# Another order of the steps of a two-branch scan on one core

## Chip, cores and metric

One core of a Trainium2 chip runs the whole kernel as one launch. The metric is the device time of one execution in microseconds, as the median of several runs.

## What is computed

One layer of a diffusion backbone on 1152 tokens (128 context, 1024 latent) of width 1024. The reference, cut to the order of its stages:

```python
h = rmsnorm(x, n1) * (1.0 + sc1) + sh1
proj = jnp.einsum('bld,de->ble', h, w_in_l).astype(jnp.float32)
# group A, 4 heads: gated linear recurrence, both directions
hg_out = head_rmsnorm(merge_heads(hg_outs[0] + hg_outs[1]), HG_HEADS, hg_norm_w_l) * jax.nn.silu(hg_g)
# group B, 4 heads: mLSTM on depthwise-convolved q/k, both directions
ml_out = head_rmsnorm(merge_heads(ml_outs[0] + ml_outs[1]), ML_HEADS, ml_norm_w_l) * jax.nn.sigmoid(ml_o)
mix = jnp.concatenate([hg_out, ml_out], axis=-1).astype(h.dtype)
x = x + g1 * jnp.einsum('ble,ed->bld', mix, w_out_l)
h = rmsnorm(x, n2) * (1.0 + sc2) + sh2
x = x + g2 * ((jax.nn.silu(h @ w_gate_l) * (h @ w_up_l)) @ w_down_l)
```

The modulation vectors sh, sc and g come from one more matrix product with the conditioning.

## The kernel before

Tokens lie in three ranges r of 384. Weights and activations are split into a high and a low part, and a product is three matmuls (`three`, line 135). The first part normalises the tokens, computes the first modulation and multiplies the first weight unit. The scan part does the eight heads and the rest of the modulation, then comes the output projection, and a long feed-forward part in two passes ends the kernel.

The first and the scan part are cut into some 130 and 450 steps, written out by hand in two lists, `ORDER0` and `ORDER` (lines 48 to 87). A loop runs each list: a step's name picks a function, which issues that step's instructions on all engines and queues. The lists set the order in which work is handed over; where a step needs a tile whose pool has no free buffer, or data that are not there, its instructions stand behind that on their engine, and the program's builder may place later steps' instructions ahead of them. Each engine then runs its own instructions in a fixed order, and so does each queue (SP for nearly all loads, POOL for the stores of head outputs).

The steps of an HGRN head (`g.h.`): zq, zf, zb, zg project one range each (24 matmuls, line 135, into tiles of that name; line 333 for the first unit); L builds decays and the scores within chunks (many small operations on DVE, tiles lv and of); KV updates the states (tile tk); O multiplies scores and states with the values (tile o) and calls `head_norm`; F calls `head_out`.

The steps of an mLSTM head (`m.h.`): zm projects q or k; cv is the convolution on DVE (tile qk); zo projects the output gate (tile og); KV updates the states (tiles mtk, C); E loads two 384 KB tiles, eb and qt, from the rows of the gates in DRAM, broadcast over the partitions (line 861, SP's queue); O1 multiplies q and k (tile ps) and turns eb into weights; O2 multiplies with values and states (tile mo, lines 891 and 893) and calls `head_norm`; F calls `head_out`. The normed tile `on` lies between the two:

```python
def head_norm(idx, r, src):
    on = s15("on" + nm, "on", 2).rearrange("p (c t) -> p c t", c=3)
    ...
def head_out(idx, r, nw, gate):
    E.transpose(pt[:, c, :], on[:, c, :], ident)
    ...
    G.dma_start(mix_d[idx, :, r * TR:(r + 1) * TR], mx)
```

`head_norm` squares on ACT, takes the root on POOL and scales on ACT (line 397). `head_out` transposes on PE (tile pt, line 405), applies weight and gate in place on DVE and stores from POOL's queue. The pool holds two `on` tiles, four Q tiles (eb and qt of the E steps) and three gate tiles, shared by zg and zo.

Other steps: vload loads and splits a weight unit for the values and vproj multiplies it (tile pv); late.k multiplies part k of the second modulation (four loads of 256 KB through two tiles wm, line 196 on PE) and lateb.k hands it on; gates is the row work for the mLSTM gates (Exp and Ln on ACT, in between Sigmoid of the heads); wo.k loads and splits row block k of the output weights, out.i.q loads head outputs and om.i.n.q multiplies them (line 984). Every first projection of a unit (zq.0, zb.0, zm.0.0, zo.0 of heads 0 and 2) and every vload issues four loads of 256 KB on SP's queue and their splits on ACT and DVE.

Of the kernel before, what the change touches and what calls it, by code (L numbers as in the profile page):

```python
# [45 lines left out]


ORDER0 = """
x.0 x.1 x.2 norm.0 norm.1 norm.2 x.3 norm.3 x.4 x.5 x.6 norm.4 raw.0 norm.5 split.0 mod.0 raw.1 mod.1 x.7
mrow.0 mod.2 h.0.0 mrow.1 h.0.1 mm.0.0.0 x.8 mm.0.0.1 mod.3 mm.0.1.1 norm.6 h.1.0 norm.7 h.1.1 split.1  # L50
mm.0.1.0 norm.8 mm.1.1.0 mrow.2 h.2.0 mod.4 raw.2 h.0.2 mm.1.0.1 mrow.3 mod.5 h.1.2 mm.0.0.2 h.2.1 h.3.2 h.3.1
mm.2.0.1 h.2.2 mm.1.1.1 mod.6 mrow.4 h.4.2 mm.2.1.1 mm.0.1.2 mm.1.1.2 h.4.0 mod.7 mrow.5 raw.3 h.4.1 h.3.0
h.5.1 mm.1.0.2 split.2 mm.2.1.2 mm.3.1.1 mm.3.0.1 mm.1.0.0 mm.2.1.0 mm.2.0.2 h.5.2 h.5.0 mrow.6 mm.2.0.0
mm.3.0.2 mm.4.0.2 h.6.1 mm.4.0.1 mm.3.1.2 split.3 mm.3.0.0 mm.3.1.0 mm.5.0.2 mrow.7 mm.4.1.0 h.6.2 h.7.2 h.6.0
mm.5.1.0 mm.4.1.2 mm.4.0.0 mm.5.0.0 mm.4.1.1 mm.5.1.1 h.7.0 mm.6.1.1 mm.5.0.1 mm.6.0.2 mm.5.1.2 mm.7.0.2
mm.6.1.2 mm.6.1.0 h.7.1 mm.6.0.1 mm.6.0.0 mm.7.0.1 mm.7.0.0 mm.7.1.2 mm.7.1.1 mm.7.1.0
"""
# [1545 lines left out]
```

## Time and profile before

| | us |
|---|---|
| median of 3 runs (1671.05 to 1676.36) | 1672.95 |
| the profiled execution | 1671.47 |
| its span, first to last instruction | 1669.7 |
| PE busy in the span | 1595.8 |
| DVE busy | 1195.0 |
| ACT busy | 694.8 |

PE is the engine of the matmuls, DVE of the elementwise work on vectors, ACT of the activations, POOL a second small vector engine, SP the queue of loads. Times in the profile count from the first instruction. A wait is named as the engine, tile and line that waited, an arrow, and what ended the wait; a line such as L135 is that of a helper, so the tile's name says which step it is.

### The profile page before, as it was taken

What the parts mean: (1) busy time and instruction counts of PE and PEld (TensorE: products, weight loads), DVE (VectorE), ACT (ScalarE), POOL (GpSimd) and SP (SyncE); (2) the same over time, 40 slices, a digit from 0 to 9 for tenths busy, and PEclk for the clock granted to TensorE, in tenths of its full rate; (3) what the DMA queues carried; (4) which work ended last, traced back from release to release, by engine and by line L of the source; (5) the groups of instructions that cost most, each with busy time, mean ns of one, the idle gap of its engine ahead of it and who ended that gap; (6) DMA issues with size and microseconds to landing.
All of it is one profiled execution on the core that took longest, in us unless ns stands there. A gap on an engine that the chain in (4) does not pass through costs nothing.

```text
span 1669.7 us, 31305 instructions
## 1 busy us (share of the span) xinstructions
PE 1595.8 (96%) x11993; PEld 1437.8 (86%) x11993; DVE 1195.0 (72%) x2620; ACT 694.8 (42%) x1656; POOL 155.5 (9%) x264
## 2 busy tenths in 40 slices
...
GB/s 316 121 24 70 83 57 88 42 72 56 77 169 50 104 90 76 96 167 191 143 184 240 214 197 200 182 191 196 183 202 233 199 232 244 256 232 239 241 207 102
DMA packets 123467, 261.53 MB, mean 157 GB/s; under 512 B 12444, under 2 KB 39476, under 8 KB 122292
## 3 DMA queue, kind: packets, MB, share of 16 engines
...
## 4 chain that ended last, share of the span: by engine, by line
PE 77%; issue 7%; DMA 6%; DVE 6%; ACT 2%; POOL 1%; SPq 0%; another core or an unknown queue 0%; DVEq 0%; POOLq 0%; ACTq 0%
PE gu L1285 27%; PE dn L135 15%; PE po L984 5%; PE zm L135 4%; PE pv L135 4%; PE zg L135 3%; PE zb L135 3%; PE zf L135 2%; DMA wm<-in_dram 2%; PE z L333 2%; PE lm L196 1%; PE zo L135 1%; DMA qt<-rows_d 1%; PE zq L135 1%; PE lv L510 1%
## 5 line engine op out<-in xcount | busy, mean ns | idle before, releaser
L135 PE MATMUL dn<-hid 128*128 128x512 f32 x1188 | 307.2, 395 | 6.6 <-ACT hid L1292 5.2
L135 PEld LDWEIGHTS dn<-hid 128*128 128x128 f32 x1188 | 214.3, 189 | 43.9 <-ACT hid L1292 6.2
L1285 PE MATMUL gu<-s,Tb 128*128 128x320 f32 (+1 forms) x1584 | 235.3, 297 | 0.6 <-ACT Tb L1096 0.4
L1285 PEld LDWEIGHTS gu<-s,Tb 128*128 128x128 f32 x1584 | 222.7, 191 | 6.3 <-ACT Tb L1096 0.7
L125 DVE TENSOR_TENSOR tmp<-gu,tmp 128x320 f32<-128x320 f32 (+1 forms) x308 | 136.0, 453 | 72.9 <-PE gu L1285 70.7
L1096 ACT CAST Tb<-r 128x512 fp32r<-128x512 f32 x176 | 106.7, 619 | 143.3 <-PE gu L1285 79.3
L1285 PE MATMUL gu<-a,Tb 128*128 128x320 f32 (+1 forms) x1056 | 156.1, 296 | 0.0
L1285 PEld LDWEIGHTS gu<-a,Tb 128*128 128x128 f32 x1056 | 148.4, 190 | 3.7
L125 DVE TENSOR_TENSOR acc<-acc,dn 128x512 f32<-128x512 f32 x172 | 117.6, 684 | 22.5 <-PE dn L135 22.5
L119 DVE TENSOR_TENSOR Tb<-r,Tb 128x512 fp32r<-128x512 f32 x176 | 119.5, 687 | 17.1 <-ACT Tb L1096 14.1
L984 PE MATMUL po<-wo_A,mix 128*128 128x512 f32 x288 | 94.2, 402 | 0.5 <-ACT mix L213 0.5
L1255 ACT CAST hid<-raw_dn 128x512 fp32r<-128x512 f32 x88 | 52.6, 617 | 74.2 <-PE dn L135 62.9
L135 PE MATMUL pv<-wh_v,h_hi 128*128 128x256 f32 (+1 forms) x288 | 82.4, 286 | 0.0
L135 PE MATMUL pv<-wh_v,h_lo 128*128 128x256 f32 (+1 forms) x288 | 81.9, 284 | 0.0
L135 PE MATMUL pv<-wl_v,h_hi 128*128 128x256 f32 (+1 forms) x288 | 81.8, 284 | 0.0
L1285 PEld LDWEIGHTS gu<-s,Tt 128*128 128x128 f32 x528 | 74.7, 189 | 4.4 <-DVE Tb L119 1.1
L1285 PE MATMUL gu<-s,Tt 128*128 128x320 f32 (+1 forms) x528 | 77.4, 296 | 0.9 <-DMA Tt<-t_d 0.9
L1285 PEld LDWEIGHTS gu<-a,Tt 128*128 128x128 f32 x528 | 74.8, 189 | 3.6 <-ACT Tb L1096 0.3
L128 DVE SCALAR_TENSOR_TENSOR qk<-pad,sm,qk 128x384 f32<-128x384 f32 (+1 forms) x144 | 77.5, 567 | 0.3
L1285 PE MATMUL gu<-a,Tt 128*128 128x320 f32 (+1 forms) x528 | 77.4, 296 | 0.1
L168 POOL TENSOR_TENSOR rs_f<-ms_f,half 128x3 f32<-128x3 f32 x24 | 25.8, 1074 | 498.2 <-DVE ms_f L166 498.2
L119 DVE TENSOR_TENSOR hid<-raw_dn,hid 128x512 fp32r<-128x512 f32 x88 | 60.2, 686 | 13.3 <-ACT hid L1255 13.3
...
## 6 DMA issues: line engine op xcount, KB each, us to landing
r<-in_dram SPq DMA_DIRECT2D x154, 256.0 KB, 3.2
...
raw_dn<-in_dram SPq DMA_DIRECT2D x88, 256.0 KB, 3.2
...
wm<-in_dram SPq DMA_DIRECT2D x64, 256.0 KB, 3.7
...
```

What stands on the lines that cost most here:

```text
L119: V.tensor_tensor(out=out, in0=a, in1=b, op=ALU.subtract)
L125: V.tensor_tensor(out=out, in0=a, in1=b, op=ALU.add)
L128: V.scalar_tensor_tensor(out=out, in0=a, scalar=s, in1=b, op0=op0, op1=op1)
L135: E.matmul(ps, a, b, start=(i == 0), stop=(i == n - 1))
L168: G.tensor_tensor(out=rs, in0=ms, in1=half[:, 0:n], op=ALU.pow)
L196: E.matmul(ps[32 * j:32 * j + 32, :], cT[:, 4 * g + j, :], rhs, start=(g == 0), stop=(g == 1), tile_position=(0, 32 * j))
L333: E.matmul(first[b][r], x, y, start=(k == 0 and n == 0), stop=(k == KD - 1 and n == 2))
L510: E.matmul(lv[32 * j:32 * j + 32, c, lev, :], kc[:, b:b + 32], diag(Q, b, m, 32 // (2 * m)), tile_position=(0, 32 * j))
L984: E.matmul(ps[n], mt[:, a, k, :], b[:, k, nn], start=(k == 0 and m == 0), stop=(k == KD - 1 and m == 2))
L1096: S.copy(hi, src)
L1255: S.copy(hi, draw[u, n])
L1285: E.matmul(ps, rt[:, x, k, :], lt[:, y, k, :], start=(n == 0), stop=(n == 11))
```

## The change

Both lists are permuted; no step is added, left out or altered. In `ORDER`, in five of sixteen places the O or O2 of a range stands ahead of the F of the range before, where that was so nowhere. The gate projections m.0.zo.2 and m.2.zo.2 stand behind F.1 of their heads, m.2.zo.1 behind the KV steps. All E steps but m.0.E.2 and m.3.E.2 stand apart from their O1. late.13 and late.14 stand together, late.15 after m.3.F.1. L and vproj of the first heads, and the early loads and products in `ORDER0`, are permuted too.

```diff
-x.0 x.1 x.2 norm.0 norm.1 norm.2 x.3 norm.3 x.4 x.5 x.6 norm.4 raw.0 norm.5 split.0 mod.0 raw.1 mod.1 x.7
...
+h.0.0 x.7 mod.2 mrow.1 h.0.1 x.8 h.1.0 mm.0.1.0 mm.0.0.0 mm.0.0.1 mm.0.1.1 norm.6 norm.7 h.1.1 mm.1.0.1 mod.3
...
 ORDER = """
...
-g.1.zb.1 g.0.O.1 pads g.1.zq.2 g.1.zb.2 g.1.zg.0 g.0.F.1 lateb.1 g.1.zg.1 late.2.B g.1.L.0 g.0.O.2 lateb.2
-g.0.F.2 g.1.zg.2 g.1.L.1 g.1.KV.0 g.2.zq.0 g.1.L.2 g.2.zf.0 late.3.B g.2.zq.1 g.1.KV.1 g.1.KV.2 g.2.zf.1
...
-vproj.1.5 m.0.cv.1.0 m.0.cv.0.2 g.2.L.1 vproj.1.2 m.0.zm.1.2 vproj.1.8 m.0.cv.1.1 g.2.KV.0 gates g.2.L.2
-g.2.KV.1 g.3.zq.0 g.3.zq.1 g.3.zq.2 m.1.zm.0.0 g.3.zf.0 late.6.B g.2.KV.2 g.3.zf.1 g.3.zf.2 m.1.zm.0.1 g.2.O.0
-g.3.zb.0 lateb.6 g.3.L.0 g.3.states g.2.F.0 g.2.O.1 late.7.B lateb.7 g.2.F.1 m.0.cv.1.2 late.8.B g.3.zb.1
...
-vproj.2.3 g.3.O.1 m.0.zo.0 g.3.F.1 g.3.O.2 m.1.cv.1.0 m.0.reload vproj.2.0 m.0.zo.1 vproj.2.1 m.0.states
-vproj.2.4 vproj.2.2 g.3.F.2 m.0.zo.2 vproj.2.6 vproj.2.5 m.0.KV.0 lateb.10 late.11.B m.1.cv.0.1 m.1.cv.0.2
-vproj.2.7 m.0.KV.1 lateb.11 vproj.2.8 m.0.KV.2 m.0.E.0 m.0.O1.0 m.0.E.1 m.0.O1.1 m.0.O2.0 m.0.F.0 m.0.O2.1
-m.0.F.1 m.1.states m.1.cv.1.1 m.0.E.2 m.0.O1.2 m.0.O2.2 m.1.zo.0 m.0.F.2 m.1.KV.0 m.1.E.0 m.1.O1.0 m.1.cv.1.2
-m.1.KV.1 m.1.zo.1 m.1.KV.2 m.2.zm.0.0 m.2.zm.0.1 m.1.O2.0 m.1.zo.2 m.2.cv.0.0 m.2.zm.0.2 vload.3 m.2.zm.1.0
-m.1.E.1 m.1.O1.1 m.2.zm.1.1 m.2.zm.1.2 m.1.F.0 m.2.cv.0.1 vproj.3.6 m.1.E.2 m.1.O1.2 m.1.O2.1 m.2.cv.1.0
-vproj.3.3 vproj.3.0 vproj.3.1 m.2.cv.1.1 m.2.zo.0 vproj.3.7 m.1.F.1 m.1.O2.2 vproj.3.8 m.2.cv.0.2 vproj.3.4
-m.1.F.2 vproj.3.5 m.2.states m.2.zo.1 m.2.cv.1.2 m.2.zo.2 vproj.3.2 m.2.KV.0 m.2.E.0 m.2.O1.0 m.3.zm.0.0
-m.2.KV.1 m.2.KV.2 m.2.O2.0 m.2.F.0 m.3.zm.0.1 m.2.E.1 m.2.O1.1 m.3.zm.0.2 m.2.O2.1 m.3.zm.1.0 m.2.E.2 m.2.O1.2
-m.3.states late.12.A m.3.cv.0.0 m.3.zm.1.1 m.2.F.1 m.3.cv.0.1 m.2.O2.2 m.3.cv.1.0 m.3.zo.0 m.3.zm.1.2 m.3.KV.0
-m.3.zo.1 m.2.F.2 m.3.zo.2 m.3.cv.0.2 lateb.12 wo.0 m.3.cv.1.1 late.13.A m.3.KV.1 m.3.E.0 m.3.O1.0 m.3.cv.1.2
-m.3.KV.2 lateb.13 late.14.A m.3.O2.0 m.3.E.1 m.3.O1.1 m.3.F.0 lateb.14 nout m.3.E.2 m.3.O1.2 late.15.A lateb.15
-wo.1 wo.2 out.0.0 wo.3 m.3.O2.1 wo.4 out.1.0 om.0.0.0 out.2.0 om.0.1.0 m.3.F.1 m.3.O2.2 om.2.1.0 out.0.1 out.2.1
-wo.5 wo.6 wo.7 om.0.0.1 om.1.1.0 m.3.F.2 om.2.1.1 out.1.1 om.1.0.0 om.0.1.1 om.1.1.1 om.2.0.0 om.2.0.1 om.1.0.1
...
+g.0.KV.1 g.1.zf.0 vproj.0.8 g.0.KV.2 lateb.0 g.1.zf.1 g.1.zb.0 g.0.O.0 late.1.B g.1.zb.1 g.1.zq.2 g.0.O.1
+g.1.zf.2 g.0.F.0 g.1.zg.0 g.1.states g.0.F.1 g.1.L.0 lateb.1 late.2.B g.0.O.2 g.2.zq.0 g.1.KV.0 g.0.F.2 g.1.L.1
...
+g.2.zq.2 g.1.O.0 g.2.zb.1 g.2.states g.1.F.0 g.2.zf.2 lateb.3 late.4.B g.2.L.0 g.1.O.1 lateb.4 g.1.O.2 late.5.B
...
+m.0.cv.0.2 m.0.cv.1.0 vproj.1.0 g.2.L.1 vproj.1.2 m.0.cv.1.1 vproj.1.8 g.2.KV.0 g.3.zq.0 gates g.3.zq.1 g.2.L.2
+g.3.zf.0 m.1.zm.0.0 g.2.KV.1 g.3.zq.2 late.6.B g.2.KV.2 g.2.O.0 g.3.zf.1 g.3.zf.2 m.1.zm.0.1 lateb.6 g.3.zb.0
+g.2.F.0 g.3.L.0 late.7.B g.2.O.1 lateb.7 m.0.cv.1.2 g.2.O.2 late.8.B g.3.zb.1 g.3.zb.2 g.2.F.1 g.3.L.1 g.2.F.2
...
+g.3.O.1 g.3.zg.2 lateb.9 m.1.zm.1.1 vload.2 m.1.zm.1.2 late.10.B vproj.2.3 g.3.F.0 m.0.zo.0 m.1.cv.0.0 g.3.F.1
+g.3.O.2 m.0.reload vproj.2.5 m.0.states m.1.cv.0.1 m.0.zo.1 g.3.F.2 vproj.2.0 vproj.2.2 vproj.2.1 vproj.2.6
+lateb.10 late.11.B m.1.cv.1.0 m.0.KV.0 m.0.E.0 vproj.2.4 m.0.E.1 m.1.cv.1.1 m.0.O1.0 m.0.O1.1 vproj.2.8
+vproj.2.7 m.0.KV.1 m.0.KV.2 m.0.O2.0 lateb.11 m.0.O2.1 m.1.states m.1.KV.0 m.1.cv.0.2 m.0.F.0 m.1.cv.1.2 m.1.E.0
+m.1.KV.1 m.0.E.2 m.0.O1.2 m.0.F.1 m.1.zo.0 m.1.zo.1 m.1.O1.0 m.0.O2.2 m.0.zo.2 m.2.zm.0.0 m.0.F.2 m.1.zo.2
+vload.3 m.1.KV.2 m.2.zm.0.1 m.2.zm.0.2 m.1.E.1 vproj.3.7 m.2.zm.1.0 m.1.O2.0 m.2.cv.0.0 m.1.O1.1 m.2.zm.1.1
+m.2.cv.1.0 m.2.zm.1.2 m.1.F.0 m.2.cv.0.1 vproj.3.6 m.1.O2.1 vproj.3.1 m.2.cv.1.1 m.1.E.2 m.2.zo.0 m.2.E.0
+vproj.3.4 m.1.F.1 vproj.3.0 m.1.O1.2 m.2.cv.0.2 vproj.3.3 m.1.O2.2 vproj.3.5 vproj.3.8 m.1.F.2 m.2.cv.1.2
+vproj.3.2 m.2.states m.2.KV.0 m.2.KV.1 m.2.KV.2 m.2.O1.0 m.2.zo.1 m.2.O2.0 m.2.E.1 m.3.zm.0.0 m.3.zm.0.1 m.2.F.0
+m.3.zm.1.0 m.2.E.2 m.2.O1.1 m.3.zm.0.2 m.2.O2.1 m.3.zo.0 m.3.states m.2.O1.2 m.3.cv.0.0 m.3.cv.0.1 m.3.E.0
+m.3.zm.1.1 m.2.F.1 m.2.zo.2 m.2.O2.2 late.12.A m.3.zm.1.2 m.3.cv.1.0 m.3.KV.0 m.2.F.2 m.3.cv.0.2 m.3.zo.1
+m.3.cv.1.1 m.3.zo.2 m.3.E.1 m.3.KV.1 lateb.12 late.13.A lateb.13 late.14.A m.3.cv.1.2 m.3.KV.2 m.3.O1.0 m.3.O2.0
+wo.0 lateb.14 nout m.3.O1.1 wo.1 m.3.F.0 out.0.0 m.3.E.2 wo.2 m.3.O1.2 wo.3 out.1.0 m.3.O2.1 om.0.1.0 wo.4
+m.3.F.1 late.15.A wo.5 out.2.0 m.3.O2.2 out.0.1 om.2.1.0 om.0.0.0 om.1.1.0 out.2.1 om.1.0.0 wo.6 wo.7 om.2.1.1
+m.3.F.2 out.1.1 lateb.15 om.0.1.1 om.0.0.1 om.2.0.0 om.2.0.1 om.1.1.1 om.1.0.1
 """
```

## Rows read from the trace of the kernel before

**Rows 1.** The page's first line, and its first part: busy us of each engine, share of the span and number of instructions.

```profile
span 1669.7 us, 31305 instructions
...
PE 1595.8 (96%) x11993; PEld 1437.8 (86%) x11993; DVE 1195.0 (72%) x2620; ACT 694.8 (42%) x1656; POOL 155.5 (9%) x264
```

**Rows 2.** Busy time by stretch. Columns: stretch in us, its length, busy us and (instructions) of PE, PEld, DVE, ACT and POOL, granted TensorE clock as a share of full speed, busy share of the DMA engines, GB/s.

```profile
0.00:67.00 67.00, 57.97 (x383) 45.06 (x384) 44.94 (x121) 42.60 (x80) 5.17 (x13) 0.95 0.66 247
67.00:500.00 433.00, 422.10 (x4621) 377.15 (x4620) 300.28 (x748) 169.17 (x467) 18.21 (x22) 1.00 0.25 75
500.00:640.00 140.00, 133.56 (x980) 129.14 (x979) 95.88 (x282) 66.78 (x213) 11.69 (x14) 1.00 0.35 82
640.00:718.00 78.00, 70.30 (x445) 65.19 (x443) 52.62 (x146) 35.25 (x109) 5.61 (x6) 0.96 0.35 81
718.00:751.00 33.00, 25.76 (x157) 15.79 (x156) 22.94 (x64) 16.89 (x50) 1.82 (x2) 0.84 0.68 198
873.00:1640.00 767.00, 755.18 (x4799) 702.43 (x4800) 581.34 (x1097) 293.09 (x578) 96.52 (x180) 0.99 0.66 215
```

**Rows 3.** Whom PE waited for over the whole span: us in total, number of waits, the longest.

```profile
PE lm L196 <- DMA wm<-in_dram: 10.3, 12, 3.5
PE pt L405 <- ACT on L397: 8.9, 6, 3.1
...
PE mo L891 <- DVE eb L128: 1.4, 1, 1.4
...
PE zm L135 <- ACT wh_mq L213: 1.1, 1, 1.1
```

**Rows 4.** The two longest stretches of the scan in which the granted clock was at its lower level; columns as in Rows 2.

```profile
689.50:696.40 6.90, 5.40 (x19) 3.25 (x20) 1.31 (x3) 0.83 (x2) 0.00 (x0) 0.51 0.32 107
737.30:747.60 10.30, 7.46 (x31) 3.99 (x32) 6.41 (x20) 5.78 (x15) 1.82 (x2) 0.50 0.83 220
```

**Rows 5.** PE in order of time (start us, us, instruction, count, [idle before it <- what ended it]): the transposes (tile pt) of g.0.F.2, m.0.F.0, m.2.F.0 and m.3.F.0, the third with the last matmuls of m.2.O2.0 (tile mo) and the last filling matmul before it.

```profile
204.51 0.33 PE L405 MATMUL pt<-con,on 128*128 128x128 f32 x1 [0.79 <-ACT on L397]
...
551.51 0.33 PE L405 MATMUL pt<-con,on 128*128 128x128 f32 x1 [1.60 <-ACT on L397]
...
666.52 0.39 PE L893 MATMUL mo<-C,qt 128*128 128x130 f32 x2
...
670.75 0.34 PE L135 MATMUL zm<-h_lo,wh_mq 128*128 128x384 f32 x1
674.18 0.33 PE L405 MATMUL pt<-con,on 128*128 128x128 f32 x1 [3.09 <-ACT on L397]
...
741.76 0.48 PE L405 MATMUL pt<-con,on 128*128 128x128 f32 x1 [1.81 <-ACT on L397]
```

**Rows 6.** The matmuls of output gates (tile zo, m.1.zo.0 and m.1.zo.1) alone, in the stretch before the transpose at 551.51. Columns: stretch, length, busy us and (instructions) of PE, PEld and ACT, clock, DMA share, GB/s.

```profile
541.70:551.50 9.80, 8.21 (x43) 7.34 (x43) 0.00 (x0) 1.00 0.64 188
```

**Rows 7.** Pieces of the chain that ended last (start us, us, what).

```profile
87.05 11.37 PE pv L135 x96
...
295.29 8.35 PE zm L135 x48
```

**Rows 8.** M.1.O2.2 (tile mo) and m.3.KV.1 (tile mtk) alone. Columns: stretch, length, busy us and (instructions) of PE, PEld, DVE and ACT, clock, DMA share, GB/s.

```profile
625.70:628.70 3.00, 2.84 (x24) 2.67 (x24) 0.98 (x6) 0.49 (x2) 1.00 0.15 57
...
719.20:722.30 3.10, 2.25 (x15) 1.82 (x15) 0.35 (x1) 1.97 (x7) 1.00 0.82 265
```

**Rows 9.** DVE in order of time, the first piece after m.2.O2.0 ended on PE.

```profile
667.97 0.61 DVE L128 SCALAR_TENSOR_TENSOR eb<-eb,ucol,con 128x128 f32<-128x128 f32 x2 [1.62 <-DMA eb<-rows_d]
```

**Rows 10.** Whom PE waited for between 540 and 720 us: us in total, times, the longest.

```profile
PE pt L405 <- ACT on L397: 6.3, 4, 3.1
```

**Rows 11.** Loads issued on SP's queue for m.2.E.2 (qt) and late.12 (wm), and PE's matmuls on wm of late.12 and late.15, each view in order of time.

```profile
680.24 0.42 SPq L861 DMA_DIRECT2D qt<-rows_d  x1
...
684.37 10.00 SPq L925 DMA_DIRECT2D wm<-in_dram  x4
...
691.00 1.07 PE L196 MATMUL lm<-wm,cT 128*32 128x256 f32 x4 [3.47 <-DMA wm<-in_dram]
...
738.33 1.62 PE L196 MATMUL lm<-wm,cT 128*32 128x256 f32 x8 [1.58 <-DMA wm<-in_dram]
```

**Rows 12.** Loads by kind: out<-in, issuing queue, count, KB each, median us from issue to landing.

```profile
wm<-in_dram SPq DMA_DIRECT2D x64, 256.0 KB, 3.7
...
qt<-rows_d SPq DMA_DIRECT2D x12, 384.0 KB, 8.0
```

**Rows 13.** One group of PE's instructions: busy us, mean ns of one, idle us before them and what ended it.

```profile
L196 PE MATMUL lm<-wm,cT 128*32 128x256 f32 x256 | 36.4, 413 | 10.8 <-DMA wm<-in_dram 10.3
```

**Rows 14.** Whom PE waited for between 718 and 752 us: us in total, times, the longest.

```profile
PE lm L196 <- DMA wm<-in_dram: 4.4, 5, 1.6
...
PE mo L893 <- DVE C L128: 0.3, 1, 0.3
```

**Rows 15.** ACT in order of time, its table loads around the gates' row work: the first and the last of five.

```profile
356.93 1.28 ACT L639 ACT_TABLE_LOAD   x1
...
383.43 1.28 ACT L442 ACT_TABLE_LOAD   x1
```

**Rows 16.** Whom SP's queue waited for between 67 and 750 us, at the loads of the E steps (line 861): us in total, times, the longest.

```profile
SPq L861 <- PE mo L893: 33.7, 7, 13.7
```

More of the change, by code (lines that the diff above doesn't have):

```diff
@@ L48 @@
 ORDER0 = """
-x.0 x.1 x.2 norm.0 norm.1 norm.2 x.3 norm.3 x.4 x.5 x.6 norm.4 raw.0 norm.5 split.0 mod.0 raw.1 mod.1 x.7
[L50 to L53, printed above, removed]
@@ L54 @@
-mm.3.0.2 mm.4.0.2 h.6.1 mm.4.0.1 mm.3.1.2 split.3 mm.3.0.0 mm.3.1.0 mm.5.0.2 mrow.7 mm.4.1.0 h.6.2 h.7.2 h.6.0
-mm.5.1.0 mm.4.1.2 mm.4.0.0 mm.5.0.0 mm.4.1.1 mm.5.1.1 h.7.0 mm.6.1.1 mm.5.0.1 mm.6.0.2 mm.5.1.2 mm.7.0.2
-mm.6.1.2 mm.6.1.0 h.7.1 mm.6.0.1 mm.6.0.0 mm.7.0.1 mm.7.0.0 mm.7.1.2 mm.7.1.1 mm.7.1.0
+x.0 x.1 x.2 norm.0 x.3 norm.1 norm.2 x.4 norm.3 x.5 norm.4 x.6 norm.5 raw.0 raw.1 split.0 mod.0 mod.1 mrow.0
+h.0.0 x.7 mod.2 mrow.1 h.0.1 x.8 h.1.0 mm.0.1.0 mm.0.0.0 mm.0.0.1 mm.0.1.1 norm.6 norm.7 h.1.1 mm.1.0.1 mod.3
@@ new lines @@
+mrow.2 norm.8 mrow.3 h.2.0 mod.4 raw.2 mm.1.1.0 h.0.2 h.1.2 h.2.1 mod.5 mm.0.0.2 split.1 h.3.1 mm.0.1.2 h.3.2
+h.2.2 mrow.4 mm.3.1.2 mod.6 mm.2.0.1 h.4.2 mm.1.1.2 h.4.1 mm.1.0.2 mm.1.1.1 mrow.5 h.4.0 mm.2.0.2 mod.7 h.5.2
+mm.2.1.1 raw.3 h.5.1 h.3.0 split.2 mm.4.0.2 mrow.6 mm.4.1.2 mm.2.0.0 h.5.0 mm.3.0.1 mm.2.1.0 mm.1.0.0 split.3
+mm.2.1.2 mm.4.0.1 mm.5.0.2 mm.3.1.1 mm.5.1.1 mm.3.0.2 mm.3.1.0 mm.5.1.2 mm.5.1.0 mrow.7 h.6.1 h.6.2 mm.4.1.1
+h.7.2 mm.4.0.0 mm.6.1.1 h.6.0 h.7.0 mm.6.0.2 mm.6.0.1 mm.5.0.0 mm.7.0.2 mm.6.0.0 h.7.1 mm.3.0.0 mm.7.0.0
@@ L57 @@
+mm.4.1.0 mm.5.0.1 mm.6.1.2 mm.7.0.1 mm.6.1.0 mm.7.1.1 mm.7.1.0 mm.7.1.2
 """
 ORDER = """
-g.0.states g.0.zb.0 vload.0 g.0.zb.1 vproj.0.0 g.0.zb.2 g.0.zg.0 vproj.0.3 vproj.0.4 vproj.0.5 vproj.0.1
-g.0.zg.1 vproj.0.2 g.0.L.0 g.0.L.1 g.0.KV.0 g.0.L.2 g.0.zg.2 vproj.0.6 g.1.zq.0 vproj.0.7 g.0.KV.1 g.1.zq.1
-late.0.B g.1.zf.0 vproj.0.8 g.0.KV.2 lateb.0 g.1.zf.1 g.1.zb.0 g.0.O.0 late.1.B g.1.zf.2 g.1.states g.0.F.0
-g.1.zb.1 g.0.O.1 pads g.1.zq.2 g.1.zb.2 g.1.zg.0 g.0.F.1 lateb.1 g.1.zg.1 late.2.B g.1.L.0 g.0.O.2 lateb.2
@@ L63 @@
-g.0.F.2 g.1.zg.2 g.1.L.1 g.1.KV.0 g.2.zq.0 g.1.L.2 g.2.zf.0 late.3.B g.2.zq.1 g.1.KV.1 g.1.KV.2 g.2.zf.1
-g.2.zb.0 lateb.3 g.2.zq.2 g.1.O.0 g.2.zf.2 g.2.zb.1 g.1.F.0 late.4.B g.2.states g.2.L.0 g.1.O.1 lateb.4 late.5.B
-g.1.F.1 g.2.zg.0 g.1.O.2 g.2.zg.1 g.2.zb.2 lateb.5 g.1.F.2 g.2.zg.2 m.0.zm.0.0 vload.1 m.0.zm.0.1 vproj.1.0
-m.0.zm.1.0 vproj.1.3 vproj.1.4 vproj.1.6 m.0.cv.0.0 m.0.zm.0.2 m.0.zm.1.1 vproj.1.7 m.0.cv.0.1 vproj.1.1
-vproj.1.5 m.0.cv.1.0 m.0.cv.0.2 g.2.L.1 vproj.1.2 m.0.zm.1.2 vproj.1.8 m.0.cv.1.1 g.2.KV.0 gates g.2.L.2
```

8 lines of the change are left out of this document (6 added, 2 removed).

## The prediction

> **What bounds the kernel now.** I read the head of the page first: PE is busy 96% of the span, the next engine, DVE, 72% [rows 1]. So the time is PE's work plus what PE loses, and the table by stretch says where that lies [rows 2]. ORDER0 fills 0 to 67 us, ORDER's scan 67 to about 787 us. From 873 to 1640 us, the feed-forward part, PE is busy 755 of 767 us, and no step of either list runs there. PE's idle time in the scan is 10.9 us from 67 to 500, 6.4 to 640, 7.7 to 718 and 7.2 to 751: 32 us of 684, denser towards the end. The list of waits gives the reasons [rows 3]: 10.3 us for the loads of the late modulation (tile wm), 8.9 us at the transposes of the heads' last steps (tile pt) for the normed tile `on`, and single waits of 1.4 and 1.1 us. The rest is many gaps below a microsecond. Last the clock: after the idle time near 687 and 738 us it is granted at 0.51 and 0.50, the lower of its two levels (1.2 against 2.4 GHz), while PE works 5.4 and 7.46 us [rows 4]. At the upper level that work takes half, so the two stretches cost 2.7 and 3.7 us. All that another order can win is thus near 32 + 6 us, 2% of the time; the work itself stays.
>
> One such wait in full: O2.0 of mLSTM head 2 ends at 666.91 us, its F.0 transposes start at 674.18, 7.3 us later; PE had zm matmuls until 671.09 and then sat 3.09 us [rows 5]. The list of before has nothing between m.2.O2.0 and m.2.F.0, and yet 4 us of zm stood there. So the list is a priority, and what is not taken as ready is passed over for later steps. The same at m.0.F.0: 8.2 us of output-gate matmuls, listed after it, ran before it [rows 6], and 1.60 us of wait remained.
>
> **The change, part by part.** No instruction and no byte is added or removed; both lists hold the same steps. The weight units (each zq.0, zb.0, zm.0.0, zo.0 and vload issues four loads) keep their order on SP's queue; E's broadcasts and the late, wo and out loads change places against them. So each part is worth the waits that it takes away or makes. Prices of cover: one projection step (24 matmuls) is 4.18 us, one vproj 2.84 us [rows 7], one O2 step 2.84, one mLSTM KV step 2.25 us [rows 8].
>
> *The second `on` tile.* Before, every F(r) precedes the next O(r+1), so one tile is in use at a time. After, five pairs are turned round (g.0, g.1, g.2, g.3, m.0). Between m.0.O2.0 and F.0 now stand O2.1 and KV.0, 5.1 us; between m.0.O2.1 and F.1 two KV and O1.2, over 4.5 us; between m.2.O2.0 and F.0 two zm, 8.4 us against the 7.3 us needed; between g.0.O.2 and F.2 some 6 us where 0.5 stood. Part of the 7.3 us was DVE standing 1.62 us for a broadcast [rows 9], and that E step now comes earlier too. So I take the waits at the transposes away: 6.3 us between 540 and 720 us [rows 10] and 0.79 at g.0.F.2, 7.1 together. The 1.81 us at m.3.F.0 [rows 5] stays: its listed cover is O1.1 alone. On POOL's queue F's write of `on` now follows the next step's rstd, which no longer queues behind it.
>
> *Output gates last, E steps first.* m.0.zo.2 and m.2.zo.2 move behind their heads' F.1, m.2.zo.1 behind the KV steps. m.2's KV steps, zo.1 and O2.0 now stand ahead of m.3.zm.0.0, where PE waited 1.1 us for the split weights, and 9.6 us stand between m.0.O1.2 and O2.2, where it waited 1.4 us for eb [rows 3]. Both go: 2.5 us.
>
> *Late modulation.* late.12 paid 3.5 us and is followed by the slow stretch: its loads were issued at 684.37, 4.1 us after a qt broadcast, and PE had the data at 691.0 [rows 11]. A broadcast has a median of 8.0 us to land, a wm load 3.7 [rows 12]. Now the broadcast next ahead (m.3.E.0) is listed a zm, a zo and an O2 step, 11.2 us, before late.12, and 18 us of other PE work stand between late.12 and late.13. I take the 3.5 us and the 2.7 us of slow clock away. late.15 moves among the output projection's matmuls, which need none of it: its 1.58 us [rows 11] goes. The Trainium skill (DMA: Bandwidth & Descriptors, Issuing engines are not separate DMA queues) says that all DMAs share the same engines and interleave. By that a broadcast moved forward delays another load instead, and the sum would be 6.2 us poorer; that is a rival below.
>
> Against these: late.13 and late.14 were 5.7 us of PE work apart and are now adjacent. Their eight loads go through two tiles, two at a time, so four rounds of 3.7 us, 14.8 us, beside two KV (4.5 us) and their own matmuls, 36.4/16 = 2.3 us each [rows 13]: up to 5.7 us more wait than none. These two already pay 4.4 - 1.6 = 2.8 us [rows 14]. I take 2.0 more, between 0 and 5.7; queued behind them on PE are m.3's KV.2, O1.0 and O2.0, and the output projection behind those.
>
> *Places that lose their cover.* g.2.KV.2 to O.0 (12.5 us to 0), m.0.KV.2 to O2.0, m.3.KV.2 to O2.0, m.3.O1.0 to O2.0 (4.6 to 0), m.3.O1.1 to O2.1, m.1.O1.2 to O2.2 (18.8 to 2.9). The nearest rows are the eb wait, 1.4 us [rows 3], and a wait of O2 for the state C, 0.3 us [rows 14]. Six places cost 0 to 8.4 us; I take 0.5 each, nearer the second, since later steps fill in: 3.0.
>
> *ORDER0.* A quarter of the first weight unit (256 KB, raw.1) now goes ahead of the first modulation load on SP's queue: at 247 GB/s [rows 2] that is 1.06 us later. PE waits for loads there, but other steps change place too: +0.5, between -1.1 and +1.1.
>
> *At nothing:* vproj, zq, zf and L change places among work that is always ready; 422.1 of 433 us are busy there [rows 2]. If that cover failed, a place costs up to the 1.4 us above. The gates' row work moves between two sigmoid steps. ACT pays five table loads of 1.28 us there already [rows 15] and is 42% busy [rows 1], so one or two more hide. The Trainium skill (ScalarE: Activation LUTs, Table sets: the hidden batching unit) says to batch functions by table set; it speaks against this move, and by it, if ACT were on the path, the sum would be 2.6 us poorer.
>
> **Sum.** Removed 7.1 + 2.5 + 3.5 + 2.7 + 1.6 = 17.4; added 2.0 + 3.0 + 0.5 = 5.5; net -11.9 us. The profiled execution took 1671.47 us (span 1669.7 and 1.8 around it), so 1659.6; the median of the runs shown, 1672.95, is 1.5 us above it: 1661.0. Bounds: half the gains and every cost in full (5.7 + 8.4 + 1.1) give +6.5; all gains with the 1.8, 2.8 and 3.7 us that I left standing, and 1.1, give -26.8.
>
> **Rivals.**
> *The broadcasts' delay moves along* (shared DMA engines): late.12's 3.5 and 2.7 us come back elsewhere; -5.7 us, 1667. For: the landing times of [rows 12]; against: the 11.2 us of PE work now listed between them exceed the 8.0. 10%.
> *The waits only move.* The list is a priority, and much of the cover was there already [rows 6]; half the gains, 8.7, less 5.5, is -3 us, 1670. 17%. *The change doesn't do what it says:* PE's order hardly differs, 1673. 5%.
> *Slower: SP's single queue.* An E step's loads need two of four Q tiles, which an O1/O2 pair gives back, and SP stood up to 13.7 us for that [rows 16]. E steps are now listed up to 38 us ahead of their O1; if one stands at SP's head, the unit weights and wm loads behind it are late, and PE runs dry. One block in full and one half covered, 13.7 + 6.9, on -11.9 is +8.7 us, 1682. It decides once such blocks pass 16.9 us of PE idle time. Against: each E is listed after the O2 that frees its tiles, with 5 to 14 us between in most cases. 15%.
>
> **How the numbers follow.** My case has 53%. A measurement of this kernel can tell about 0.3%, 5 us: faster is below 1668, slower above 1678. Faster is 0.53 + 0.10 = 0.63, same 0.17 + 0.05 = 0.22, slower 0.15. My own case reaches from 1649 (most of the -26.8) to 1668; with the two near-zero rivals the range goes up to 1677, which leaves out most of the slower case and the far end of the gains. The predicted time is my case's, 1661.
>
> **What would show it.** Right: the transposes' wait for `on` falls from 8.9 us to under 3; no wait above 1.5 us at late.12 and no slow clock near 690 us; idle time of 67 to 751 us down from 32 to some 22 us; feed-forward spans unchanged. Wrong: new waits above 2 us at O2 for eb or C, at late.13 and late.14, or of projections for split weights with SP standing at E's loads; a longer slow stretch before the output projection; or more than 2 us lost before 67 us.

## The result and the profile after

The changed kernel takes 1661.26 us (median of 5 runs, 1657.22 to 1665.51), beside 1672.95 us (5 runs, 1667.61 to 1676.36) of the kernel before: 0.9933 of it, 95% interval 0.9910 to 0.9956. In a second set of runs, beside other runs of before, it was 0.9942 (0.9924 to 0.9960). The profiled execution took 1657.22 us, the fastest of the five, so its span of 1655.4 us shows more gain (14.3 us) than the medians do (11.7).

The head of the changed kernel's page, which answers [rows 1]:

```profile
span 1655.4 us, 31292 instructions
...
PE 1586.9 (96%) x11993; PEld 1434.6 (87%) x11993; DVE 1196.2 (72%) x2620; ACT 696.3 (42%) x1657; POOL 152.0 (9%) x264
```

PE has the same 11,993 matmuls and is still busy 96%, yet its busy time fell by 8.9 us. To see where, I cut both spans at the same events: the end of the first unit's products (z), the end of the last output product (om), the end. First before, then changed; columns as in [rows 2].

```profile
0.00:67.46 67.46, 58.43 (x385) 45.52 (x386) 44.94 (x121) 43.05 (x81) 5.17 (x13) 0.95 0.66 247
67.46:787.06 719.60, 687.31 (x6368) 616.76 (x6367) 489.27 (x1281) 300.56 (x872) 41.37 (x50) 0.99 0.31 89
787.06:1669.70 882.64, 850.06 (x5245) 775.57 (x5242) 660.76 (x1218) 351.20 (x704) 108.93 (x201) 0.99 0.63 205
```

```profile
0.00:64.42 64.42, 55.63 (x385) 42.50 (x386) 44.88 (x120) 43.95 (x83) 5.16 (x13) 1.00 0.69 257
64.42:775.17 710.75, 681.73 (x6365) 616.34 (x6364) 490.81 (x1283) 300.48 (x871) 38.05 (x50) 0.99 0.31 88
775.17:1655.40 880.23, 849.56 (x5244) 775.73 (x5244) 660.51 (x1218) 351.88 (x704) 108.80 (x201) 0.99 0.63 207
```

The scan part (second row) is 8.9 us shorter, the first part 3.0, the rest 2.4. In the scan part PE's idle time fell by only 3.3 us (32.3 to 29.0), its busy time by 5.6. Whom PE waited for in the changed scan part, to be read against [rows 3]:

```profile
PE lm L196 <- DMA wm<-in_dram: 9.2, 10, 3.5
PE mo L891 <- DVE eb L128: 4.4, 2, 3.9
PE lv L510 <- DVE Q L122: 4.2, 10, 1.5
PE po L984 <- DVE wo_B L119: 1.4, 1, 1.4
PE po L984 <- ACT mix L213: 1.0, 1, 1.0
PE pt L405 <- ACT C L847: 1.0, 1, 1.0
PE pt L405 <- DVE dn L898: 0.9, 1, 0.9
...
PE pt L405 <- ACT on L397: 0.7, 1, 0.7
...
PE po L984 <- ACT wo_A L960: 0.5, 1, 0.5
```

The transposes (pt) wait 2.6 us where they waited 8.9. The wait for the wm loads stayed near 10, those for eb tripled, and the output projection (po) waits 2.9 us in the scan part, where none of its waits was on the list before. Three stretches of the scan part ran at the lower clock:

```profile
617.10:620.50 3.40, 2.92 (x13) 2.92 (x14) 0.91 (x4) 0.13 (x1) 0.00 (x0) 0.50 0.14 58
688.70:695.50 6.80, 5.91 (x21) 3.76 (x22) 1.63 (x5) 2.50 (x7) 0.00 (x0) 0.50 0.44 125
739.90:746.70 6.80, 6.24 (x26) 5.13 (x27) 1.95 (x5) 2.85 (x7) 0.60 (x1) 0.50 0.53 177
```

The first comes with the eb wait, the second with late.12's, as before [rows 4]; the third stands where 10.3 us stood before.

Below I split each scan part into PE's idle time, the cost of the slow clock (half of what PE worked at the lower level) and PE's busy time at the full clock, all summed from the traces, so that the three add up to its length. Before: 32.3, 8.1 and 679.2 us; changed: 29.0, 7.6 and 674.1. So 5.1 of the 8.9 us are busy time.

### The profile page after: what moved, and what is told of

The parts are those of the page before. It is cut to its first block, busy times and chain, and to the rows that moved or that the text cites. A ratio compares the mean times of both kernels' runs of the same rounds, so it can differ in the third digit from the quotient of the medians.

```text
span 1655.4 us, 31292 instructions
## 1 busy us (share of the span) xinstructions
PE 1586.9 (96%) x11993; PEld 1434.6 (87%) x11993; DVE 1196.2 (72%) x2620; ACT 696.3 (42%) x1657; POOL 152.0 (9%) x264
## 4 chain that ended last, share of the span: by engine, by line
PE 80%; DVE 7%; DMA 6%; issue 3%; ACT 2%; POOL 1%; SPq 0%; another core or an unknown queue 0%; DVEq 0%; POOLq 0%; ACTq 0%
PE gu L1285 28%; PE dn L135 16%; PE pv L135 5%; PE po L984 5%; PE zm L135 5%; PE zg L135 3%; PE zb L135 2%; DMA qt<-rows_d 2%; PE zo L135 2%; DMA wm<-in_dram 2%; PE zq L135 2%; PE zf L135 2%; PE z L333 2%; PE lm L196 1%; PE mo L891 1%
## 5 line engine op out<-in xcount | busy, mean ns | idle before, releaser
L119 DVE TENSOR_TENSOR hid<-raw_dn,hid 128x512 fp32r<-128x512 f32 x88 | 60.3, 688 | 11.7 <-ACT hid L1255 11.7
```

Source lines behind the costliest of these rows:

```text
L119: V.tensor_tensor(out=out, in0=a, in1=b, op=ALU.subtract)
```

## The experiments

Ratios are to the kernel before, run on the same chip; the last four columns are us in one profile of each kernel. `ORDER0` has 114 steps and `ORDER` 320.

| kernel | ratio (95%) | scan part | idle | slow clock | busy at full clock |
|---|---|---|---|---|---|
| before | 1 | 719.6 | 32.3 | 8.1 | 679.2 |
| changed | 0.9933 (0.9910 to 0.9956) | 710.8 | 29.0 | 7.6 | 674.1 |
| e9, changed again | 0.9942 (0.9924 to 0.9960) | 711.1 | 27.9 | 7.8 | 675.4 |
| e1, front only | 0.9998 (0.9983 to 1.0013) | 721.7 | 31.4 | 11.9 | 678.4 |
| e8, first half | 0.9955 (0.9940 to 0.9970) | 717.4 | 30.6 | 13.6 | 673.2 |
| e12, second half | 1.0010 (0.9998 to 1.0022) | 717.8 | 32.1 | 4.1 | 681.6 |
| e5, pairs only | 1.0007 (0.9994 to 1.0020) | 720.9 | 32.8 | 8.9 | 679.2 |
| e2, changed, pairs back | 0.9992 (0.9975 to 1.0009) | 716.8 | 33.0 | 6.3 | 677.5 |
| e3b, changed, late.12 moved | 0.9920 (0.9902 to 0.9939) | 712.6 | 29.0 | 9.0 | 674.6 |
| e4, changed, O2.2 moved | 0.9930 (0.9914 to 0.9945) | 707.0 | 27.5 | 6.1 | 673.4 |
| e7, changed, late.12 at a broadcast | 0.9930, one run | 711.2 | 27.2 | 9.2 | 674.7 |
| e6, changed, four moves | 0.9936 (0.9914 to 0.9957) | 708.6 | 26.3 | 8.1 | 674.2 |
| e10, before, five late steps moved | 1.0004 (0.9989 to 1.0018) | 726.8 | 35.8 | 13.7 | 677.3 |
| e11, changed, two mends and five late steps | 0.9926 (0.9914 to 0.9938) | 707.7 | 28.8 | 1.5 | 677.4 |

**e1, the front alone.** `ORDER0` changed, `ORDER` as before.

```diff
-x.0 x.1 x.2 norm.0 norm.1 norm.2 x.3 norm.3 x.4 x.5 x.6 norm.4 raw.0 norm.5 split.0 mod.0 raw.1 mod.1 x.7
...
+x.0 x.1 x.2 norm.0 x.3 norm.1 norm.2 x.4 norm.3 x.5 norm.4 x.6 norm.5 raw.0 raw.1 split.0 mod.0 mod.1 mrow.0
...
```

> The kernel before with only ORDER0 replaced by the changed one; ORDER as before. In the two profiles the first part ended at 67.5 us before and 64.4 us after, and the 6.8 us of slow clock from 23.9 us on were there before and not after. Theory A (ORDER0 is worth about nothing, +0.5 us as I had put it; the slow stretch at 24 us comes or not by chance): the median stays at 1673 (1670 to 1676), and a first part that ends early does so only where the profile shows no slow stretch near 24 us. Rival B (the new ORDER0 itself keeps the clock up and is worth 3 us): the first part ends at 64.4 us again, no slow clock before 40 us, the median is 1670. In both the scan keeps its long waits: 3.1 us at m.2.F.0, 3.5 us at late.12, some 9 us at the transposes in all.

The median does not differ from before, and a slow stretch of 3.4 us came back, at 13.9 us. The first part ended at 65.4 us. Over all profiles, first parts without slow clock ended at 66.1 us with the old `ORDER0` (e5) and at 64.2 to 65.0 with the new one (e7, e8, e9, e11 and the first profile); with 6.8 us of slow clock, at 67.5 and 68.4 (before, e10) and 67.3 (e4). So the new list is worth about 1 us, the clock up to 3, and the clock comes by chance: the same list ran with and without the slow stretch. A holds, but for that 1 us.

**e8 and e12, the two halves.** `ORDER0` and the steps up to m.0.KV.0 from one order, the others from the other. Where e8 goes over, against the changed kernel:

```diff
-lateb.10 late.11.B m.1.cv.1.0 m.0.KV.0 m.0.E.0 vproj.2.4 m.0.E.1 m.1.cv.1.1 m.0.O1.0 m.0.O1.1 vproj.2.8
...
+lateb.10 late.11.B m.1.cv.1.0 vproj.2.4 m.0.zo.2 m.0.KV.0 m.1.cv.0.2 vproj.2.7 m.0.KV.1 lateb.11 vproj.2.8
```

> ORDER0 and the steps of ORDER up to m.0.KV.0 as in the changed kernel (the HGRN heads, projections, late.0 to late.11), all later steps in the order of before. The changed kernel's scan part is 8.9 us shorter. Theory A (half of it comes from the HGRN heads, where PE has 3.4 to 5 us less busy time for the same matmuls, and the long waits of the mLSTM heads make up the other half): scan part 714 to 717 us, median 1664 to 1667, with the waits of 3 us at m.2.F.0 and of 3.5 us at late.12 and the slow clock of 10 us near 737 us as before. Rival B (all comes from the mLSTM heads): scan part 718 to 721 us, median 1669 to 1672. Rival C (all comes from the HGRN heads): 710 to 712 us, 1660 to 1662.

> The other half of the change: ORDER0 and the steps up to m.0.KV.0 as before, all later steps in the changed order. With the first half alone the scan part was 717.4 us, 6.7 us ahead of before up to m.2.zm.0.0, of which it gave back 4.5 in the last 90 us. Theory A (the halves add up; the second half wins its 3 to 4 us at the transposes and E steps of m.0, and loses at m.1.O2.2 what it wins at m.2.F.0): PE's start of m.2.zm.0.0 stays within 4 us of before's, scan part 714 to 718 us, median 1665 to 1669. Rival B (the second half is worth nothing without the first): scan part 719 to 721 us. The wait of 4 us at m.1.O2.2 and that of 3.5 us at late.12 come in both; the transposes wait less than 3 us in all, against 8.9.

The first half alone gives 7.4 us (medians 1662.28 and 1669.67), nearly what C gave it, though the waits at m.2.F.0 (2.9 us) and late.12 (2.9) are there as in A. Its profile shows less, a scan part of 717.4 us, just above A's: the profiled execution is the slowest of its eight (1666.20), with 13.6 us lost to slow clock. The second alone has A's scan part and B's median, 1670.73: nothing that can be told from none. PE between the end of z and the end of m.2.zm.0.0, e8 and then before:

```profile
65.03:557.15 492.12, 477.61 (x5078) 434.81 (x5078) 336.71 (x867) 196.72 (x555) 21.14 (x28) 1.00 0.24 76
```

```profile
67.46:566.33 498.87, 483.32 (x5078) 435.47 (x5078) 336.91 (x865) 196.45 (x556) 22.76 (x28) 1.00 0.25 75
```

It is 6.7 us over the same 5,078 matmuls, 5.7 of them busy time and 1.0 idle; both have 3.4 us of slow clock in it. Behind it e8's profile gives 4.5 us back. What the second half does alone shows in e12's waits:

```profile
PE lm L196 <- DMA wm<-in_dram: 8.0, 10, 4.0
PE mo L891 <- DVE eb L128: 5.2, 2, 4.2
PE mtk L833 <- ACT mkt L827: 3.3, 3, 2.5
PE pt L405 <- ACT on L397: 2.7, 5, 0.8
```

The transposes' waits are gone as I had said (2.7 us of 8.9), and waits for eb and for the copied keys (mkt) stand in their place.

**e2 and e5, the five pairs.** Turned back in the changed kernel, and turned in the kernel before; one of the five:

```diff
-lateb.11 m.0.O2.1 m.1.states m.1.KV.0 m.1.cv.0.2 m.0.F.0 m.1.cv.1.2
+lateb.11 m.1.states m.1.KV.0 m.1.cv.0.2 m.0.F.0 m.0.O2.1 m.1.cv.1.2
...
-m.0.O2.0 m.0.F.0 m.0.O2.1
+m.0.O2.0 m.0.O2.1 m.0.F.0
```

> The changed kernel with the five turned pairs turned back: g.0.O.1, g.1.O.2, g.2.O.2, g.3.O.1 and m.0.O2.1 stand right behind the F of the range before, so that one normed tile is in use at a time as before. Theory A (the waits at the transposes went because other work was listed between O2 and F, not because of the second tile): only m.0.F.0 loses cover, one O2 step of 2.8 us; its wait grows from 0.9 to at most 3.7 us, all other transposes wait under 1 us, the median is 1661 to 1665. Rival B (the second tile is what removed them, 7.1 us in my sum): the transposes wait for 6 us or more in all, 1667 to 1668.

> The kernel before with the five pairs turned and nothing else: O or O2 of the next range directly ahead of the F (g.0.O.1, g.1.O.2, g.2.O.2, g.3.O.1, m.0.O2.1). Turning them back in the changed kernel made its scan part 6 us longer in the profile (716.8 against 710.8 us) and its median some 8 us, with the transposes' own wait only 0.6 us up. Theory A (the turned pairs bring PE ready work earlier wherever they stand): the scan part of the kernel before falls from 719.6 to 712 to 716 us, the median to 1664 to 1668. Rival B (the pairs are worth something only beside the changed kernel's other moves, which need O's work at those places): the scan part stays at 718 to 721 us; of the waits only that at m.0.F.0 (1.6 us) goes, and the median stays within 3 us of before.

Turning them back costs nearly the whole gain (0.9992), which neither theory gave by its own mechanism: the transposes' waits rise as A said, to 3.2 us in all, but the rest of the loss is elsewhere. Between 540 and 630 us of e2:

```profile
PE mo L891 <- DVE eb L128: 6.5, 2, 4.6
PE pt L405 <- ACT on L397: 2.3, 2, 1.8
```

m.0.O2.2 now waits 2.0 us for eb, wm waits are 11.3 us in all against 9.2, and the busy time is 3.4 us up. Turned alone in the kernel before, the pairs give nothing (e5, B), and the transposes wait longer than the 8.9 us of before, where B had the 1.6 us at m.0.F.0 gone:

```profile
PE pt L405 <- ACT on L397: 9.7, 7, 3.0
```

So the pairs are worth something only beside the other moves, and not at the transposes.

**e3b and e7, late.12.** In e3b it stands four steps earlier, ahead of m.3.E.0 and away from any broadcast (m.3.zm.1.1 goes ahead of m.3.E.0 too); in e7 directly behind m.2.O2.1, where m.2.E.2's broadcasts are issued.

```diff
-m.3.cv.0.0 m.3.cv.0.1 m.3.E.0 m.3.zm.1.1 m.2.F.1 m.2.zo.2 m.2.O2.2 late.12.A m.3.zm.1.2
+m.3.cv.0.0 m.3.cv.0.1 m.3.zm.1.1 late.12.A m.3.E.0 m.2.F.1 m.2.zo.2 m.2.O2.2 m.3.zm.1.2
...
+m.2.O2.1 late.12.A m.3.zo.0 m.3.states
```

> The changed kernel with late.12 listed ahead of m.3.E.0 and behind m.3.zm.1.1, two steps earlier; nothing else moves. In the changed kernel m.3.E.0's broadcast of eb, listed 11 us before late.12, was issued only at 681.95 us, when m.2.O2.2 gave its tile back, and the two wm loads at 682.74 us landed between the two broadcasts at 689.5. Theory A (the wm loads of late.12 are late because they share the DMA engines with the broadcasts issued beside them): with the loads issued at about 675 us, 7 us before the next broadcast, late.12 waits under 1 us (from 3.5), the slow clock of 6.8 us near 690 us is gone, and the run is 5 to 6 us shorter, 1655 to 1657. Rival B (two wm tiles with one round of loads under 4 us of other work always cost this): late.12 still waits 2 us or more, 1660 to 1662. Rival C (the delay moves to m.3.E.0 and its O1.0): late.12 waits little, but new waits of 3 us or more come at m.3.O1.0, O2.0 or late.13.

> The changed kernel with late.12 directly behind m.2.O2.1, where its second pair of loads is issued just as m.2.E.2's broadcasts of eb and qt are, which wait for the tiles that m.2.O2.1 gives back. Theory A (the loads are late because of the broadcasts beside them): late.12 waits 2.5 us or more there, as at its old place, and slow clock follows within 10 us; at the place two steps later, away from any broadcast, it waited 0.5 us. Rival B (what helped was only the earlier place): late.12 waits under 1 us here too.

SP's issues in the changed kernel around late.12, then in e7 and in e3b:

```profile
681.95 0.36 SPq L861 DMA_DIRECT2D eb<-rows_d  x1
682.74 0.82 SPq L925 DMA_DIRECT2D wm<-in_dram  x2
683.61 0.42 SPq L861 DMA_DIRECT2D qt<-rows_d  x1
```

```profile
666.37 0.36 SPq L861 DMA_DIRECT2D eb<-rows_d  x1
667.16 0.82 SPq L925 DMA_DIRECT2D wm<-in_dram  x2
668.03 0.42 SPq L861 DMA_DIRECT2D qt<-rows_d  x1
```

```profile
671.60 0.42 SPq L861 DMA_DIRECT2D qt<-rows_d  x1
...
680.99 5.28 SPq L925 DMA_DIRECT2D wm<-in_dram  x4
690.15 0.38 SPq L861 DMA_DIRECT2D eb<-rows_d  x1
```

In the first two the wm loads go out between two broadcasts, in e3b 9 us from either. PE's wait at late.12 in the changed kernel, in e7 and in e3b (in brackets):

```profile
689.59 1.07 PE L196 MATMUL lm<-wm,cT 128*32 128x256 f32 x4 [3.54 <-DMA wm<-in_dram]
```

```profile
672.54 0.63 PE L196 MATMUL lm<-wm,cT 128*32 128x256 f32 x4 [2.03 <-DMA wm<-in_dram]
...
674.55 1.06 PE L196 MATMUL lm<-wm,cT 128*32 128x256 f32 x4 [0.84 <-DMA wm<-in_dram]
```

```profile
684.16 0.63 PE L196 MATMUL lm<-wm,cT 128*32 128x256 f32 x4 [0.45 <-DMA wm<-in_dram]
```

Beside a broadcast late.12 waits 3.5 and 2.9 us and 6.8 us of slow clock follow (from 688.7, in e7 from 674.0); away from one 0.45 us, with none at that place. Nor is it the time since the issue: PE goes on 6.9 and 5.4 us after the first wm load beside a broadcast, 3.2 us after it in e3b. The same move in e6 and e11 leaves no wait above 0.6 us there either. The Trainium skill (DMA: Bandwidth & Descriptors, Issuing engines are not separate DMA queues) says that transfers share the same engines and interleave; these three traces agree. At late.12 e3b gains 5.2 us against the changed kernel, and then m.3.KV.2 waits for its convolution, at 711 us:

```profile
711.14 0.52 PE L824 MATMUL mtk<-con,qk 128*128 128x128 f32 x3 [2.19 <-DVE qk L128]
```

Of the 5.2 us, 2.2 remain at the end of the scan part, which in this profile is still 1.9 us longer than the changed kernel's: before late.12 it had lost 4 us elsewhere, to slow clock at 378 and 620 us above all. A names the cause. C is right that half of the gain moves on, though not to the steps that it named.

**e4, the place that lost its cover.**

```diff
-vproj.3.3 m.1.O2.2 vproj.3.5 vproj.3.8 m.1.F.2 m.2.cv.1.2 vproj.3.2 m.2.states m.2.KV.0 m.2.KV.1 m.2.KV.2
+vproj.3.3 vproj.3.5 vproj.3.8 m.1.O2.2 m.2.cv.1.2 vproj.3.2 m.2.states m.2.KV.0 m.2.KV.1 m.2.KV.2 m.1.F.2
```

> The changed kernel with m.1.O2.2 listed two vproj steps (5.7 us) later, behind vproj.3.8, and m.1.F.2 behind m.2.KV.2, so that it keeps its cover; nothing else moves. In the changed kernel PE waited 3.9 us for eb at m.1.O2.2 and then ran 3.4 us at the slow clock, which at half speed costs 1.7 us. Theory A (the place lost its cover, 18.8 us of listed PE work before and 2.9 after, and this is the whole cause): the wait falls below 0.5 us, the slow stretch near 617 us goes, 5 to 5.6 us are won, 1656. Rival B (eb is late for the steps behind it as well; the wait moves to m.1.F.2 or to m.2's O1.0 or KV): the wait reappears within the next 20 us at 2 us or more, 1659 to 1661.

In the changed kernel DVE stood 3.7 us for m.1.E.2's broadcast, issued at 599.39 us, with the convolutions of m.2 queued behind it, and PE paid 3.9 us (each in brackets):

```profile
608.80 0.96 DVE L122 TENSOR_TENSOR qt<-qt,qk 128x768 f32<-128x768 f32 x1 [3.68 <-DMA qt<-rows_d]
```

```profile
617.58 0.80 PE L891 MATMUL mo<-v,eb 128*128 128x130 f32 x2 [3.93 <-DVE eb L128]
```

In e4 PE's list for 600 to 640 us holds no wait for eb, and no slow clock:

```profile
PE mtk L824 <- DVE C L128: 1.3, 1, 1.3
PE mtk L833 <- ACT mkt L827: 1.0, 1, 1.0
```

The scan part is 3.8 us shorter, some 3 of it here. A, less 1.3 us that m.2.KV.2 takes back by waiting for its states. By the ratios e4 can't be told from the changed kernel.

**e9, the changed kernel again.**

> The changed kernel as it is, beside the other kernels on the same chip. Scan part 710 to 713 us, the wait of 3.5 to 4.5 us at m.1.O2.2 and that of 3.5 us at late.12 again (the kernels with one of them mended still had the other), median 0.993 of before. If the 4 us by which the profiled run lay under its median came of the clock in the first part alone, a profile with a slow stretch near 25 us has a first part of 66 to 67.5 us and the same scan part.

As expected, with 4.3 us at m.1.O2.2 and 3.9 at late.12. Its first part took 65.0 us without slow clock.

**e6, four moves together.** e3b and e4, and

```diff
-m.3.KV.1 lateb.12 late.13.A lateb.13 late.14.A m.3.cv.1.2 m.3.KV.2
+m.3.cv.1.2 m.3.zo.2 m.3.E.1 m.3.KV.1 lateb.12 late.13.A lateb.13 late.14.A m.3.KV.2
...
-m.3.F.1 late.15.A wo.5
+m.3.F.2 out.1.1 late.15.A om.0.1.1 om.0.0.1 lateb.15
```

> The changed kernel with both mends, late.12 ahead of m.3.E.0 (worth 5.2 us at its place and some 2 at the end) and m.1.O2.2 two vproj steps later with m.1.F.2 behind m.2.KV.2 (worth 3 us), and two more moves: m.3.cv.1.2 behind m.3.cv.1.1, ahead of m.3.KV.1 (in the run with late.12 moved PE waited 2.2 us for it), and late.15 behind out.1.1 among the last products of the output projection (it waited 1.4 us, and 6.8 us of slow clock followed). Theory A (each mend keeps its worth beside the others): scan part 702 to 705 us against 710.8, median 1650 to 1654 on a chip where the changed kernel has 1660. Rival B (what is won goes to the next wait, since DVE and the loads set the pace of the last 70 us): scan part 707 to 710 us, median 1656 to 1659, with new waits of 2 us or more between 690 and 775 us.

B: by the ratio nothing is left of the two mends, and the scan part is 2 us shorter, not 6 to 9. From 700 to 775 us:

```profile
PE po L984 <- ACT wo_A L960: 3.2, 2, 2.6
PE mtk L824 <- DVE qk L128: 2.7, 1, 2.7
PE lm L196 <- DMA wm<-in_dram: 2.0, 2, 1.6
```

**e10 and e11, the late steps.** In both, five late steps stand beside L, KV and F steps; e11 has e3b and e4 as well. One of each:

```diff
-g.1.zq.1 late.0.B
+g.0.L.1 late.0.B
...
-g.2.O.2 late.8.B
+g.3.L.2 late.8.B
```

> The kernel before with five steps of the late modulation listed elsewhere: late.0 behind g.0.L.1, late.4 behind g.2.L.0, late.7 behind g.3.L.0, late.9 behind g.3.L.2, late.10 behind g.3.F.0; nothing else moves. With it PE goes 12 times from a projection to a late matmul and 13 times back, against 19 and 24 before and 11 and 16 in the changed kernel. In the traces such a step in takes 0.29 us from start to start and a step back 0.31, against 0.18 from projection to projection and 0.07 and 0.10 between a late matmul and the scores of an L step, so a visit costs 0.26 us more (0.293 + 0.309 + 0.010 - 0.07 - 0.10 - 0.18). Theory A (a part of the gain of the first half is that late matmuls stand beside L and O steps and not beside projections): 7 to 11 such visits fewer, PE's busy time in the scan at full clock 1.8 to 2.9 us less than before's 679.5, median 1 to 3 us below before. Rival B (the busy time does not depend on the neighbours, it is waits too short to be listed): busy time at full clock stays at 679 to 680 us.

> The changed kernel with late.12 ahead of m.3.E.0, m.1.O2.2 two vproj steps later with m.1.F.2 behind m.2.KV.2, and five late steps beside L, KV and F steps (late.1 behind g.0.F.1, late.2 behind g.0.F.2, late.6 behind g.2.KV.2, late.8 behind g.3.L.2, late.10 behind g.3.F.1), which takes the visits of late matmuls from projections from 11 to 8 and back from 16 to 9. m.3.cv.1.2 and late.15 stay where the changed kernel has them (moving them gave new waits of 2.7 and 2.6 us). Theory A: 2 us from late.12, 3 us from m.1.O2.2, 1 to 1.5 us of busy time; scan part 704 to 707 us against 710.8 and 711.1, median 5 to 6 us below the changed kernel, ratio to before 0.990. Rival B (DVE and the loads set the pace from 690 us on and take back what comes before): scan part 708 to 711 us, ratio 0.993 to 0.995.

e10's busy time falls by 1.9 us, as A had it, but its waits for wm rise to 12.6 us, and the median stays. e11 speaks against A: with still fewer such visits than the changed kernel its busy time is 2.0 to 3.3 us higher. Its scan part, 707.7 us, and its ratio lie between what A and B gave. So the neighbours of the late matmuls don't settle the busy time. With 0.9926 e11 may beat the changed kernel (medians 1656.98 and 1660.07, a study apart); the intervals overlap, and so do those of e3b.

## Why the prediction was right, and where it was not

The number, 1661.0 us, was right within 0.3 us, the side too, but not the sum behind it: that it fits so well is luck. The sum gave the scan part -12.4 us, and the profile has -8.9, with terms off by up to 6 us both ways; the first part and the rest, which it gave +0.5 and 0, have -3.0 and -2.4 in that one profile. And the largest real term was not in it.

*The step that failed* is in what bounds the kernel: "All that another order can win is thus near 32 + 6 us, 2% of the time; the work itself stays", and with it "At nothing: vproj, zq, zf and L change places among work that is always ready". The first half, where they lie beside four of the five turned pairs and the late steps, brought most: 7.4 us in e8. The same 5,078 matmuls cost 5.7 us less busy time, and it is no scatter: in the scan part at full clock 679.2, 678.4 and 679.2 us in three kernels with the old order or only the pairs turned (before, e1, e5) and 681.6 with the old first half (e12), but 673.2 to 675.4 in seven with the new first half (changed, e9, e8, e3b, e4, e6, e7). With its pairs turned back (e2) or late steps moved (e11) it is 677.5 and 677.4, and the old order with late steps moved (e10) has 677.3. Which of its moves the gain hangs on is thus not shown. The page's busy time runs to a modelled end of each matmul; here in the changed kernel the second starts 0.18 us after the first, which is shown 0.34 us long:

```profile
683.10 0.34 PE L135 MATMUL zm<-h_hi,wl_mq 128*128 128x384 f32 x1
683.28 0.34 PE L135 MATMUL zm<-h_hi,wh_mq 128*128 128x384 f32 x1
```

So slower steps between kinds of matmul and waits shorter than that tail are counted as busy.

*The second `on` tile* (7.1 us): the waits fell by 6.3 us, nearly as said. But by e12 and e2 that is not where the time was won: the list of waits shrinks at pt and grows at eb, mkt and po. For the second half the rival that the waits only move was right.

*Output gates last, E first* (2.5): both waits went as said, the 1.1 us for the split weights and the 1.4 us of m.0.O2.2 for eb: between 540 and 600 us PE waits for one transpose only, 1.0 us. The 4.4 us for eb in the list above are two others, 3.9 us at m.1.O2.2, counted below at the six places, and 0.5 us after 670.

*late.12* (6.2): nothing came; 3.54 us and 5.91/2 of slow clock remained. I reckoned with the place of m.3.E.0 in the list, 11.2 us ahead; its eb load waited for the tile that m.2.O2.2 gave back and went out beside the wm loads (e3b, e7). *late.15* (1.6): it still waits 1.4 us, a gain of 0.2. *The stretch before the output projection*, which I left standing, fell from 10.2 to 6.8 us of slow clock, a gain of 0.6 (7.46/2 to 6.24/2).

*late.13 and late.14* (+2.0): 1.9 us of waits against 2.8, so -0.9; the matmuls between the rounds seem to have covered more than I counted. *Six places without cover* (+3.0): one paid for all, m.1.O2.2 with 3.9 and 1.5 us (e4), the others half a microsecond at most. *ORDER0* (+0.5): about -1, and up to 3 of clock that comes by chance (e1). *Feed-forward* (0): 879.0 to 885.5 us over all profiles without a relation to the order, but for e6 at the top, whose late.15 stood close to it.

*At nothing, the gates:* ACT has one table load more, six instead of five between 350 and 384 us, and PE's waits at the gates' rows are 1.0 us instead of 1.4. The Trainium skill (ScalarE: Activation LUTs, Table sets: the hidden batching unit) says to batch functions by table set. The move went against that and cost nothing that shows here: no wait of PE between 345 and 385 us ended with ACT, so the 2.6 us that I had named did not come.

Of the signs that I had named, the transposes are under 3 us as said; late.12 above 1.5 us, idle time of 29 instead of some 22 us and the new wait for eb are the wrong ones.

*The slower rival:* SP stood up to 14.0 us at an E step's loads, about as before [rows 16], and no projection ran dry for it:

```profile
SPq L861 <- DVE eb L128: 27.9, 4, 14.0
```

What stays open is the source of the 5.7 us. Counted by which kind of matmul follows which, each at its median step, the new neighbours explain 2.0 to 2.3 us, by how finely kinds are told apart; the others are steps longer than their kind's median, spread over many kinds, and e11 shows that the late steps alone do not govern them.
